# Decay levels of a linear attention: 64 stationary columns, the two halves of the partitions written in turn

## The chip, the cores and the metric

One core of a Trainium2 chip. The metric is the device time of one execution in microseconds (us), taken over several runs of the same program. Engines are named as in the profile: PE is TensorE, PEld its weight load, DVE is VectorE, ACT is ScalarE, POOL is GpSimd, SP is the engine whose queue issues most DMAs.

## What is computed

A decoder trunk of two layers over 256 tokens of width 2048. Layer 0 mixes tokens with a gated linear attention, layer 1 with a forgetting softmax attention; each layer also attends to 256 memory tokens and ends with a gated MLP of width 5632. The change touches the linear attention alone. Cut to that, the reference is:

```python
def step(state, inp):                       # one chunk of 64 tokens, 4 chunks, 4 heads, dk = 256
    qc, kc, vc, gc = inp
    bcum = jnp.cumsum(gc, axis=2)
    o_inter = jnp.einsum('bhtk,bhkv->bhtv', qc * jnp.exp(bcum), state)
    rel = bcum[:, :, :, None, :] - bcum[:, :, None, :, :]
    decay = jnp.exp(jnp.where(tri, rel, -jnp.inf))
    att = jnp.einsum('bhtk,bhsk,bhtsk->bhts', qc, kc, decay)
    o_intra = jnp.einsum('bhts,bhsv->bhtv', att, vc)
```

Each product of a query and a key inside a chunk has a decay of its own for every one of the 256 key channels, so `att` isn't one matrix product.

## The kernel before, in words

All large products are weight projections: weights stream in as units of up to 128 x 1024 floats, ACT rounds each unit to the matmul format (`whi`, line 190), DVE makes the rest (`wlo`, line 199), and PE multiplies both with the activations. Lines 224, 225 and 227 are the products of a projection whose output stands feature by feature (`proj_fm`), lines 261 to 263 those of one whose output stands token by token (`proj_tm`). `split_unit` gives the two casts a high priority; otherwise a scheduler with a cost model of its own lays out one order for each engine, and PE runs its instructions in that order.

The linear attention (`gla`) takes four heads in turn. For each head the projections of q, k and v are followed by `core`, whose work the scheduler spreads between the projections of the next heads. `core` builds the transposed attention matrix `at` (keys on the 128 partitions, queries along the columns) out of these parts, all in plain 32-bit floats:

- line 548: products of the later with the earlier half of the tokens, 128 stationary columns;
- line 552: products of neighbouring chunks inside a half `b` of the tokens, 64 stationary columns, all written to partitions 0 to 63;
- line 557: plain products of each 128-token block with itself, 128 stationary and 128 moving columns, of which line 562 keeps the diagonal by a predicated copy with the identity as mask;
- line 588, for each of three decay levels (`LEVELS`, blocks of 64, 16 and 4 tokens): a block is cut in four, and three versions of the decayed queries (`VERSIONS`, made at lines 572 to 575 as `gdd`) are multiplied with the keys decayed to the end of their quarter (`ks`, lines 581 to 583). The moving side holds the versions of both chunks of a 128-token block, 192 columns (`NVER`), against 128 stationary key columns. Line 595 picks the valid entries with three predicated copies for each level, by a 0/1 mask that `_constants` lays out.

A plain 32-bit matmul is recorded in the profile as two passes, each with a weight load of its own. [...] Lines 602 and 603 multiply `at` with v.

Of the kernel before, what the change touches and what calls it, by code (L numbers as in the profile page):

```python
# [12 lines left out]
F32 = mybir.dt.float32  # L13
F32R = mybir.dt.float32r
I32 = mybir.dt.int32
AF = mybir.ActivationFunctionType
# [3 lines left out]
P = 128  # L20
T = 256
# [9 lines left out]
BIG = 1e30  # L31
PARTS = ((0, 16), (16, 32), (32, 44))

LEVELS = (64, 16, 4)
VERSIONS = ((0, 96), (96, 64), (160, 32))
NVER = 192
NUNIT = 1024
AHEAD = 300

# [97 lines left out]
def _trunk(ctx: ExitStack, tc: tile.TileContext, xt, xtok, memt, wp, wgu, gns, gfin, cnv, par, msk, out):  # L137
    nc = tc.nc
    where, _ = _layout()
    V, S, TE = nc.vector, nc.scalar, nc.tensor  # L140
# [13 lines left out]
    ident = mask[:, M_ID : M_ID + P]  # L154
# [314 lines left out]
    def gla(nx):  # L469
        h, mix = bufB, bufA  # L470
        with tc.tile_pool(name="gla", bufs=1) as gp:
# [53 lines left out]
            def core(hd, q, k, v, bc):  # L525
                at = att[hd % 2]
                e1 = gp.tile([P, 2, T], F32, name="ge1", tag="ed", bufs=2)
                d1 = gp.tile([P, 2, T], F32, name="gd1", tag="ed", bufs=2)
                q1 = gp.tile([P, 2, T], F32, name="gq1", tag="gq1")
                k1 = gp.tile([P, 2, T], F32, name="gk1", tag="gk1")  # L530
                et = sm.tile([P, 2, 2], F32, name="get", tag="get")
                S.activation(et, bc[:, :, 127:192:64], AF.Exp, scale=1.0 / TAU)
                S.activation(e1[:, :, :192], bc[:, :, 64:], AF.Exp, scale=1.0 / TAU)
                V.tensor_tensor(q1[:, :, :192], q[:, :, 64:], e1[:, :, :192], ALU.mult)
                b4 = bc.rearrange("p d (c t) -> p d c t", t=64)
                d4 = d1.rearrange("p d (c t) -> p d c t", t=64)
                V.tensor_tensor(d4[:, :, :3, :], b4[:, :, :3, 63:64].to_broadcast([P, 2, 3, 64]), b4[:, :, :3, :],
                                ALU.subtract)
                S.activation(d1[:, :, :192], d1[:, :, :192], AF.Exp, scale=1.0 / TAU)
                V.tensor_tensor(k1[:, :, 192:], k[:, :, :64], d1[:, :, :64], ALU.mult)  # L540
                V.tensor_tensor(k1[:, :, 64:192], k[:, :, 64:192], d1[:, :, 64:192], ALU.mult)
                for c in range(2):
                    V.tensor_scalar(k1[:, c, :64], k1[:, c, 192:], et[:, c, 0:1], None, ALU.mult)
                    V.tensor_scalar(q1[:, c, 192:], q1[:, c, 128:192], et[:, c, 1:2], None, ALU.mult)
                ps = work("s", 2)
                for c in range(2):
                    mov = q1[:, c, :].rearrange("p (n t) -> p n t", t=64)[:, 1:4:2, :]
                    TE.matmul(ps[:, :P], k1[:, c, :P], mov, start=c == 0, stop=c == 1)
                for b in range(2):
                    for c in range(2):  # L550
                        lhs = k1[:, c, 128:192] if b else k1[:, c, 192:]
                        TE.matmul(ps[:64, P + 64 * b : P + 64 * (b + 1)], lhs, q1[:, c, P * b : P * b + 64],
                                  start=c == 0, stop=c == 1)
                for b in range(2):
                    for c in range(2):
                        bs = slice(b * P, (b + 1) * P)
                        TE.matmul(ps[:, T + b * P : T + (b + 1) * P], k[:, c, bs], q[:, c, bs],  # L557
                                  start=c == 0, stop=c == 1)
                a3 = at.rearrange("p (b t) -> p b t", t=P)[:, 0:3:2, :]
                S.activation(at[:, P : 2 * P], ps[:, :P], AF.Copy)  # L560
                S.activation(a3[:64, :, 64:], ps[:64, P : 2 * P].rearrange("p (b t) -> p b t", t=64), AF.Copy)
                V.copy_predicated(a3, ident.bitcast(I32).unsqueeze(1).to_broadcast([P, 2, P]),
                                  ps[:, T:].rearrange("p (b t) -> p b t", t=P))
                for li, B in enumerate(LEVELS):
                    H = B // 4
                    ps = work("s", 2)
                    dd = gp.tile([P, 4, NVER], F32, name="gdd", tag="gdd")
                    b4, q4 = (t.rearrange("p d (b n t) -> p (d b) n t", b=2, t=B) for t in (bc, q))
                    parts = [(dd[:, :, o : o + w].rearrange("p a (n t) -> p a n t", t=(3 - i) * H), (i + 1) * H)
                             for i, (o, w) in enumerate(VERSIONS)]  # L570
                    for d, t0 in parts:
                        V.tensor_tensor(d, b4[:, :, :, t0:], b4[:, :, :, t0 - 1 : t0].to_broadcast(d.shape), ALU.subtract)
                    S.activation(dd, dd, AF.Exp, scale=1.0 / TAU)
                    for d, t0 in parts:
                        V.tensor_tensor(d, d, q4[:, :, :, t0:], ALU.mult)
                    if H > 1:
                        kt = ks[li % 2]
                        de = gp.tile([P, 2, T], F32, name="gde", tag="ed", bufs=2)
                        b5, k5, e5, kt5 = (t.rearrange("p d (n r t) -> p (d n) r t", r=4, t=H)[:, :, :3, :]
                                           for t in (bc, k, de, kt))  # L580
                        V.tensor_tensor(e5, b5[:, :, :, H - 1 :].to_broadcast(e5.shape), b5, ALU.subtract)
                        S.activation(e5, e5, AF.Exp, scale=1.0 / TAU)
                        V.tensor_tensor(kt5, k5, e5, ALU.mult)
                    else:
                        kt = k
                    for b in range(2):
                        for c in range(2):
                            TE.matmul(ps[:, b * NVER : (b + 1) * NVER], kt[:, c, b * P : (b + 1) * P],  # L588
                                      dd[:, 2 * c + b, :], start=c == 0, stop=c == 1)
                    p3 = ps[:, : 2 * NVER].rearrange("p (b c) -> p b c", b=2)  # L590
                    m3 = mask[:, M_LVL + NVER * li : M_LVL + NVER * (li + 1)].bitcast(I32)
                    for i, (o, w) in enumerate(VERSIONS):
                        o4 = a3.rearrange("p b (n t) -> p b n t", t=B)[:, :, :, (i + 1) * H :]
                        m4 = m3[:, o : o + w].rearrange("p (n t) -> p n t", t=(3 - i) * H).unsqueeze(1)
                        V.copy_predicated(o4, m4.to_broadcast(o4.shape),
                                          p3[:, :, o : o + w].rearrange("p b (n t) -> p b n t", t=(3 - i) * H))
                nrm = Norm(DV, "o")
                os = []
                for j in range(3):
                    po = work("o")  # L600
                    vs = slice(j * P, (j + 1) * P)
                    TE.matmul(po[:, :T], v[:, 0, vs], at[:, :T], start=True, stop=False)  # L602
                    TE.matmul(po[:, P:T], v[:, 1, vs], at[:, T:], start=False, stop=True)
                    o = gp.tile([P, T], F32, name="onorm", tag="onorm", bufs=9)
                    on[3 * hd + j] = o
                    S.activation(o, po[:, :T], AF.Copy)
                    nrm.add(o)
                    os.append(o)
                for j, o in enumerate(os):
                    f = C_GN + 3 * hd + j  # L610
                    V.scalar_tensor_tensor(o, o, part[:, f : f + 1], nrm.row(), ALU.mult, ALU.mult)
# [12 lines left out]
            for hd in range(GLA_H):  # L624
                bc = gates(hd)
                q = gp.tile([P, 2, T], F32, name="gq", tag="gq", bufs=2)
                k = gp.tile([P, 2, T], F32, name="gk", tag="gk", bufs=2)
# [175 lines left out]
    n, then = preparing("ffn0", bufB)  # L803
# [52 lines left out]
def _constants():  # L856
    m = np.zeros((P, M_N), np.float32)
    r = np.arange(P)
    m[:, M_ID : M_ID + P] = np.eye(P)
    m[:, M_ONE : M_ONE + P] = 1.0  # L860
    m[:, M_FOX + P : M_FOX + T] = np.where(r[None, :] > r[:, None], BIG, 0.0)
    m[:, M_SCAN : M_SCAN + T] = np.where(np.arange(T) % 64 == 0, 0.0, 1.0)[None, :]
    for li, B in enumerate(LEVELS):
        for i, (o, w) in enumerate(VERSIONS):
            seg = np.arange(w) // ((3 - i) * B // 4)
            c = M_LVL + NVER * li + o
            m[:, c : c + w] = (r[:, None] // B == seg[None, :]) & (r[:, None] % B // (B // 4) == i)
    return m


# [49 lines left out]
```

## Time and profile before

| | |
|---|---|
| median of 3 runs | 2309.28 us (2309.21 to 2309.69) |
| profiled execution, own time | 2308.97 us |
| its span | 2307.2 us |
| PE busy | 2289.1 us, 12256 passes |
| DVE busy | 1605.6 us |
| ACT busy | 1251.5 us |
| granted PE clock | 0.999 |
| stretch of the linear attention's `core` | about 181 to 400 us |

The page gives busy time by engine, the time in slices, the chain of work that ended last (followed back from the last instruction to what released it) and the costliest groups of instructions. In the group rows, "128\*128 128x192 f32" is a stationary operand of 128 rows and 128 columns, and an output of 128 partitions by 192 columns. In the chain, a row is a start in us, a length in us, engine, tile and line, and the number of passes: the lengths add up without overlap, so the length over the number of passes is the pitch at which passes follow each other, while a pass's own duration in the other views includes the time in the pipe.

### The profile page before, as it was taken

What the parts mean: (1) busy time and instruction counts of PE and PEld (TensorE: products, weight loads), DVE (VectorE), ACT (ScalarE), POOL (GpSimd) and SP (SyncE); (2) the same over time, 40 slices, a digit from 0 to 9 for tenths busy, and PEclk for the clock granted to TensorE, in tenths of its full rate; (3) what the DMA queues carried; (4) which work ended last, traced back from release to release, by engine and by line L of the source; (5) the groups of instructions that cost most, each with busy time, mean ns of one, the idle gap of its engine ahead of it and who ended that gap; (6) DMA issues with size and microseconds to landing.
All of it is one profiled execution on the core that took longest, in us unless ns stands there. A gap on an engine that the chain in (4) does not pass through costs nothing.

```text
span 2307.2 us, 32826 instructions
## 1 busy us (share of the span) xinstructions
PE 2289.1 (99%) x12256; PEld 1986.0 (86%) x12256; DVE 1605.6 (70%) x2595; ACT 1251.5 (54%) x1954; POOL 3.0 (0%) x19
## 2 busy tenths in 40 slices
PE   8999999999999999999999999999999999999998
PEld 7889998888888888888888998888888888888886
DVE  7567877577774777557767557657776577756775
ACT  6555555455553555445565455556554455534554
POOL 0000000000000000000000000000000000000000
PEclk9999999999999999999999999999999999999999
DMA  8655455655555555655555564565556555565554
GB/s 305 204 161 158 147 163 166 192 185 185 190 192 191 192 186 189 192 192 191 187 186 184 172 207 151 163 198 183 191 186 192 194 187 191 186 196 190 186 191 155
DMA packets 124744, 430.27 MB, mean 186 GB/s; under 512 B 14108, under 2 KB 18600, under 8 KB 124456
## 3 DMA queue, kind: packets, MB, share of 16 engines
q1 hardware_dynamic: 124296, 427.65, 57.6%
q8 instruction: 96, 1.57, 0.3%
q10 hardware_dynamic: 288, 0.52, 0.1%
q14 instruction: 64, 0.52, 0.1%
HBM read 426.01 MB, written 2.11 MB: 186 GB/s over the span
## 4 chain that ended last, share of the span: by engine, by line
PE 98%; DMA 0%; ACT 0%; DVE 0%; issue 0%; SPq 0%; DVEq 0%; ACTq 0%
PE acc L224 37%; PE acc L225 20%; PE acc L262 12%; PE acc L263 12%; PE acc L261 12%; PE acc L227 2%; PE ps_s L588 1%; PE ps_s L794 0%; PE ps_t L379 0%; PE ps_s L386 0%; PE ps_o L397 0%; DMA mt<-memt 0%; PE ps_s L708 0%; PE ps_o L602 0%; PE ps_o L724 0%; PE ps_s L557 0%
## 5 line engine op out<-in xcount | busy, mean ns | idle before, releaser
L199 DVE TENSOR_TENSOR wlo<-raw,whi 128x1024 fp32r<-128x1024 f32 (+4 forms) x809 | 972.6, 1203 | 554.1 <-ACT whi L190 541.4
L190 ACT ACTIVATE whi<-raw 128x1024 fp32r<-128x1024 f32 (+4 forms) x809 | 843.2, 1043 | 779.6 <-PE acc L263 366.6
L224 PE MATMUL acc<-B,whi 128*128 128x512 f32 x1980 | 683.4, 395 | 0.0
L224 PE MATMUL acc<-A,whi 128*128 128x512 f32 x1680 | 580.6, 396 | 7.4 <-ACT whi L190 7.4
L225 PE MATMUL acc<-B,wlo 128*128 128x256 f32 x2112 | 551.4, 281 | 0.0
L225 PE MATMUL acc<-A,wlo 128*128 128x256 f32 x1792 | 464.5, 281 | 0.5 <-DVE wlo L199 0.5
L224 PEld LDWEIGHTS acc<-B,whi 128*128 128x128 f32 x1980 | 361.0, 188 | 68.3
L225 PEld LDWEIGHTS acc<-B,wlo 128*128 128x128 f32 x2112 | 397.6, 188 | 20.8
L224 PEld LDWEIGHTS acc<-A,whi 128*128 128x128 f32 x1680 | 305.8, 188 | 64.0 <-ACT whi L190 7.7
L225 PEld LDWEIGHTS acc<-A,wlo 128*128 128x128 f32 x1792 | 338.1, 189 | 21.0 <-DVE wlo L199 1.2
L262 PE MATMUL acc<-wlo,B 128*128 128x512 f32 (+3 forms) x736 | 275.4, 374 | 1.2 <-DVE wlo L199 1.2
L263 PE MATMUL acc<-whi,B 128*128 128x512 f32 (+3 forms) x736 | 273.7, 372 | 0.0
L261 PE MATMUL acc<-whi,B 128*128 128x512 f32 (+3 forms) x736 | 247.8, 372 | 0.0
L262 PE MATMUL acc<-wlo,A 128*128 128x512 f32 x544 | 212.4, 390 | 0.0
L263 PE MATMUL acc<-whi,A 128*128 128x512 f32 x544 | 212.0, 390 | 0.0
L261 PE MATMUL acc<-whi,A 128*128 128x512 f32 x544 | 192.8, 391 | 0.0
L232 ACT ACTIVATE part<-acc 128x256 f32<-128x256 f32 x240 | 90.1, 375 | 165.4 <-PE acc L227 165.4
L262 PEld LDWEIGHTS acc<-wlo,B 128*128 128x128 f32 x736 | 138.2, 188 | 20.6 <-DVE wlo L199 1.5
L263 PEld LDWEIGHTS acc<-whi,B 128*128 128x128 f32 x736 | 138.2, 188 | 18.9
L261 PEld LDWEIGHTS acc<-whi,B 128*128 128x128 f32 x736 | 137.4, 188 | 18.7
L234 DVE TENSOR_TENSOR wholes<-acc,part 128x256 f32<-128x256 f32 x240 | 101.0, 421 | 67.4 <-ACT part L232 67.3
L263 PEld LDWEIGHTS acc<-whi,A 128*128 128x128 f32 x544 | 102.1, 188 | 21.2
(196 smaller groups left out, 1576.1 us busy)
## 6 DMA issues: line engine op xcount, KB each, us to landing
raw<-wp SPq DMA_DIRECT2D x743, 512.0 KB, 3.4
raw<-wp SPq DMA_DIRECT2D x32, 384.0 KB, 3.1
raw<-wp SPq DMA_DIRECT2D x24, 388.0 KB, 3.1
raw<-wp SPq DMA_DIRECT2D x8, 400.0 KB, 3.1
xf<-xt SPq DMA_DIRECT2D x16, 128.0 KB, 4.7
x<-xtok SPq DMA_DIRECT2D x4, 512.0 KB, 7.1
mt<-memt SPq DMA_DIRECT2D x3, 512.0 KB, 7.8
cb<-cdram SPq DMA_DIRECT2D x12, 128.0 KB, 3.4
```

What stands on the lines that cost most here:

```text
L190: casts.append(S.activation(hi[:, s], raw[:, s], AF.Copy))
L199: V.tensor_tensor(lo[:, s], raw[:, s], hi[:, s].bitcast(F32), ALU.subtract)
L224: TE.matmul(a, hi[:, s], both, start=done == 0, stop=False)
L225: TE.matmul(a[:, :T], lo[:, s], both[:, 0, :], start=False, stop=False)
L227: TE.matmul(a, hi[:, s], both, start=False, stop=True)
L232: S.activation(t, a[:, T:], AF.Copy)
L234: V.tensor_tensor(r, a[:, :T], t, ALU.add)
L261: TE.matmul(a, xk[:, 0, xs], hi[:, s], start=u == 0 and j == 0, stop=False)
L262: TE.matmul(a, xk[:, 0, xs], lo[:, s], start=False, stop=False)
L263: TE.matmul(a, xk[:, 1, xs], hi[:, s], start=False, stop=last)
L588: TE.matmul(ps[:, b * NVER : (b + 1) * NVER], kt[:, c, b * P : (b + 1) * P], dd[:, 2 * c + b, :], start=c == 0, stop=c == 1)
```

## The change

Lines 548 and 602 stay. The parts at lines 552, 557 and 588 now use 64 stationary columns throughout, and consecutive matmuls write partitions 0 to 63 and 64 to 127 in turn. A 64-token chunk of keys meets only the decayed queries of its own chunk, so a level's moving side has 96 columns and not 192, and there are eight matmuls where there were four. The diagonal has eight matmuls of 64 moving columns where it had four of 128. The four products of neighbouring chunks keep their size; the second block's go to the upper partitions, and the loops over `b` and `c` are exchanged. Behind them, each predicated copy becomes two of 64 partitions (for a level six in place of three), and the ACT copy of line 561 becomes two. The masks shrink from 192 to 96 columns a level. The decayed queries have the same number of elements, cut as 8 x 96 and not 4 x 192.

```diff
 LEVELS = (64, 16, 4)
-VERSIONS = ((0, 96), (96, 64), (160, 32))
-NVER = 192
+VERSIONS = ((0, 48), (48, 32), (80, 16))
+NVER = 96
...
-                for b in range(2):
-                    for c in range(2):
+                for c in range(2):
+                    for b in range(2):
                         lhs = k1[:, c, 128:192] if b else k1[:, c, 192:]
-                        TE.matmul(ps[:64, P + 64 * b : P + 64 * (b + 1)], lhs, q1[:, c, P * b : P * b + 64],
+                        TE.matmul(ps[64 * b : 64 * (b + 1), P : P + 64], lhs, q1[:, c, P * b : P * b + 64],
                                   start=c == 0, stop=c == 1)
                 for b in range(2):
                     for c in range(2):
-                        bs = slice(b * P, (b + 1) * P)
-                        TE.matmul(ps[:, T + b * P : T + (b + 1) * P], k[:, c, bs], q[:, c, bs],
-                                  start=c == 0, stop=c == 1)
+                        for g in range(2):
+                            gs = slice(b * P + 64 * g, b * P + 64 * (g + 1))
+                            TE.matmul(ps[64 * g : 64 * (g + 1), T + b * 64 : T + (b + 1) * 64], k[:, c, gs], q[:, c, gs],
+                                      start=c == 0, stop=c == 1)
...
-                S.activation(a3[:64, :, 64:], ps[:64, P : 2 * P].rearrange("p (b t) -> p b t", t=64), AF.Copy)
-                V.copy_predicated(a3, ident.bitcast(I32).unsqueeze(1).to_broadcast([P, 2, P]),
-                                  ps[:, T:].rearrange("p (b t) -> p b t", t=P))
+                for b in range(2):
+                    S.activation(a3[:64, b, 64:], ps[64 * b : 64 * (b + 1), P : P + 64], AF.Copy)
+                for g in range(2):
+                    gs = slice(64 * g, 64 * (g + 1))
+                    og = a3[gs, :, gs]
+                    V.copy_predicated(og, ident[gs, gs].bitcast(I32).unsqueeze(1).to_broadcast(og.shape),
+                                      ps[gs, T : T + P].rearrange("p (b t) -> p b t", t=64))
...
-                    dd = gp.tile([P, 4, NVER], F32, name="gdd", tag="gdd")
-                    b4, q4 = (t.rearrange("p d (b n t) -> p (d b) n t", b=2, t=B) for t in (bc, q))
+                    dd = gp.tile([P, 8, NVER], F32, name="gdd", tag="gdd")
+                    b4, q4 = (t.rearrange("p d (g n t) -> p (d g) n t", g=4, t=B) for t in (bc, q))
...
                     for b in range(2):
                         for c in range(2):
-                            TE.matmul(ps[:, b * NVER : (b + 1) * NVER], kt[:, c, b * P : (b + 1) * P],
-                                      dd[:, 2 * c + b, :], start=c == 0, stop=c == 1)
+                            for g in range(2):
+                                TE.matmul(ps[64 * g : 64 * (g + 1), b * NVER : (b + 1) * NVER],
+                                          kt[:, c, b * P + 64 * g : b * P + 64 * (g + 1)],
+                                          dd[:, 4 * c + 2 * b + g, :], start=c == 0, stop=c == 1)
...
                     for i, (o, w) in enumerate(VERSIONS):
                         o4 = a3.rearrange("p b (n t) -> p b n t", t=B)[:, :, :, (i + 1) * H :]
-                        m4 = m3[:, o : o + w].rearrange("p (n t) -> p n t", t=(3 - i) * H).unsqueeze(1)
-                        V.copy_predicated(o4, m4.to_broadcast(o4.shape),
-                                          p3[:, :, o : o + w].rearrange("p b (n t) -> p b n t", t=(3 - i) * H))
+                        for g in range(2):
+                            gs = slice(64 * g, 64 * (g + 1))
+                            n = 64 // B
+                            og = o4[gs, :, g * n : (g + 1) * n, :]
+                            m4 = m3[gs, o : o + w].rearrange("p (n t) -> p n t", t=(3 - i) * H).unsqueeze(1)
+                            V.copy_predicated(og, m4.to_broadcast(og.shape),
+                                              p3[gs, :, o : o + w].rearrange("p b (n t) -> p b n t", t=(3 - i) * H))
```

More of the change, by code (lines that the diff above doesn't have):

```diff
@@ L866, in _constants @@
             c = M_LVL + NVER * li + o
-            m[:, c : c + w] = (r[:, None] // B == seg[None, :]) & (r[:, None] % B // (B // 4) == i)
+            m[:, c : c + w] = (r[:, None] % 64 // B == seg[None, :]) & (r[:, None] % B // (B // 4) == i)
     return m
```

## The prediction

> **What bounds the kernel now.** I read the page first: the busy times, then the chain that ended last.
>
> ```profile
> span 2307.2 us, 32826 instructions
> PE 2289.1 (99%) x12256; PEld 1986.0 (86%) x12256; DVE 1605.6 (70%) x2595; ACT 1251.5 (54%) x1954; POOL 3.0 (0%) x19
> ...
> PE 98%; DMA 0%; ACT 0%; DVE 0%; issue 0%; SPq 0%; DVEq 0%; ACTq 0%
> ```
>
> PE is busy for 99% of the span and is 98% of the chain. Next come PE's waits, over the whole span, and the busy times of the stretch in which the changed code runs.
>
> ```profile
> engine line waited for: us in total, times, longest us
> PE acc L224 <- ACT whi L190: 7.4, 1, 7.4
> PE acc L262 <- DVE wlo L199: 1.2, 1, 1.2
> PE acc L225 <- DVE wlo L199: 0.5, 1, 0.5
> ...
> 181.00:400.00 219.00, 219.00 (x1287) 199.66 (x1286) 174.44 (x386) 121.68 (x206) 0.00 (x0) 1.00 0.50 157
> ```
>
> The columns of the last row are PE, PEld, DVE, ACT and POOL, then the granted clock (1.00). From 181 to 400 us PE has no gap, and none of the three waits is in the changed code. So a nanosecond of PE in `core` is a nanosecond of the end, and the question is what the new matmuls cost PE. The chain, asked for single stretches, prices the old ones (start us, length us, passes):
>
> ```profile
> 181.84 0.45 PE ps_s L548 x4
> 182.29 0.61 PE ps_s L552 x8
> 182.90 1.09 PE ps_s L557 x8
> 183.98 1.30 PE ps_s L588 x8
> 194.00 1.30 PE ps_s L588 x8
> ...
> 225.62 0.49 PE ps_s L552 x6
> 226.12 0.64 PE ps_t L315 x4
> 226.76 0.26 PE ps_s L552 x2
> 227.01 1.09 PE ps_s L557 x8
> ...
> 329.19 0.26 PE ps_s L552 x2
> 329.45 0.38 PE acc L262
> 329.83 0.17 PE acc L263
> ...
> 334.28 0.38 PE ps_s L552 x4
> ...
> 363.36 1.30 PE ps_s L588 x8
> ```
>
> A level (line 588) is 1.30 us for 8 passes of 192 moving columns: 0.1625 a pass. Line 548 gives 0.45 / 4 = 0.112 for 128 stationary and 128 moving columns. Line 552 (64 and 64) gives (0.49 - 0.26) / 4 = 0.0575 from its stretches of 6 and 2 passes. That leaves 0.61 - 8 x 0.0575 = 0.15 and 0.26 - 2 x 0.0575 = 0.145 over: the price of coming into 64 columns. Going out costs too: 1.09 - 8 x 0.112 = 0.19 at line 557, 0.64 - 0.45 = 0.19 at line 315, 0.38 - 0.17 = 0.21 at a projection. A visit to 64 columns thus costs 0.145 + 0.195 = 0.34 us. The passes show half of why:
>
> ```profile
> L552 PE MATMUL ps_s<-gq,gk x32: 222/222/270, 182.2 to 334.4; 128*64 128x64 f32 x32
> L557 PE MATMUL ps_s<-gq,gk x32: 272/275/377, 182.8 to 341.8; 128*128 128x128 f32 x32
> L588 PEld LDWEIGHTS ps_s<-gdd,ks x64: 187/190/192, 183.7 to 354.1; 128*128 128x128 f32 x64
> ```
>
> Durations are minimum, median, maximum in ns. The longest is the first pass behind a switch, which shows its weight load: 270 - 222 = 48 ns for 64 columns, 377 - 275 = 102 for 128. In the rest of the visit, 0.34 - 0.15 = 0.19, no pass starts, half of it on the way in and half on the way out. Inside a level no load shows: loads of 190 ns lie under passes that follow each other every 162.5 ns.
>
> **The change, part by part.**
>
> *Visits.* Before has seven stretches of 64 columns (the chain's rows of line 552, the first at 182.29, the last at 334.28). In the built order of the changed kernel there are 20: three for head 0, four each for heads 1 and 2, nine for head 3, where the scheduler puts projection matmuls between the diagonal and the first level's products. 13 more at 0.34: +4.4 us. This is the surest term, since PE keeps its program order.
>
> *Levels.* A level becomes 16 passes of 96 moving columns. Between 0.0575 at 64 and 0.1625 at 192 the line gives 0.083 at 96. If the halves run one after another, 16 x 0.083 = 1.33 us, +0.03 a level, +0.3 for the 12. If passes of different halves run at the same time, two share a slot of 0.083; the two passes of a matmul go to the same half and queue, so the first of them and the last have no partner: 9 slots, 0.75 us, -0.55 a level, -6.6 in all.
>
> *Diagonal.* 16 passes of 64 and 64 for 8 of 128 and 128: one after another 0.92 against 0.90, +0.1 over four heads; side by side 9 x 0.0575 = 0.52, -0.38 each, -1.5.
>
> *Products of neighbouring chunks.* 8 passes as before; side by side 5 x 0.0575 = 0.29 against 0.46, -0.7 over four heads; else nothing.
>
> No row of before shows two halves at work together, as line 552 writes the lower one alone. So the parts on PE lie between +4.4 + 0.4 = +4.8 us and +4.4 - 6.6 - 1.5 - 0.7 = -4.4 us. With no slot lost at the ends it would be +4.4 - 12 x 0.65 - 4 x 0.45 - 4 x 0.23 = -6.1. With no gain in the two small parts, where load and pass are equally long, +4.4 - 6.6 = -2.2. I take -4.4. [...]
>
> [...]
>
> *DVE and ACT.* 40 predicated copies become 80.
>
> ```profile
> L595 DVE COPY_PREDICATED att<-mask,ps_s 128x192 f32<-128x192 int32 x12 | 4.8, 398 | 4.9 <-PE ps_s L588 4.9
> L595 DVE COPY_PREDICATED att<-mask,ps_s 128x64 f32<-128x64 int32 x12 | 3.6, 298 | 0.1
> L562 DVE COPY_PREDICATED att<-mask,ps_s 128x256 f32<-128x256 int32 x4 | 1.8, 442 | 2.5 <-ACT att L561 2.5
> L561 ACT ACTIVATE att<-ps_s 64x128 f32<-64x128 f32 x4 | 1.0, 258 | 0.0
> 189.13 1.09 DVE L575 TENSOR_TENSOR gdd<-gdd,gq 128x384 f32<-128x384 f32 x3
> ```
>
> 100 ns for 128 more columns: an added copy costs at most its fixed part, 298 - 50 = 0.25 us, so 40 x 0.25 = 10 us is the upper end, added to 174.44 busy in 219. It hides. The queries of head 0's second level are ready at 189.13 + 1.09 = 190.2 and PE reaches them at 194.0: 3.8 us of slack, against 3 x 0.25 = 0.75 more for the copies of the level ahead of them. In the DVE queue the casts (`wlo`) and the next level's subtractions stand behind the copies; PE waits for `wlo` nowhere in this stretch. The four added ACT copies are at most 0.26 us each. If this cover failed, each level could give back up to 0.75 us, 9 us in all; I take nothing. The smaller masks shorten one early load that is none of PE's three waits. Behind `core` the built order is the same.
>
> **The sum.** Against the profiled execution, 2308.97 us: 2308.97 - 4.4 = 2304.6. The median of the runs is 0.31 higher, so 2304.9. That is -0.19%; 0.2%, about what a measurement of this kernel can tell from no change, is 4.6 us.
>
> **The rivals.**
>
> *One after another (slower).* The halves never overlap: a pass of one half starts when the pass of the other has been fed. Then the visits are unpaid: 2309.3 + 4.8 = 2314.1, and up to 2316.5 if PE also waits a little at head 3. It decides from the point where a level, its visit left out, takes more than 1.30 - 4.4 / 12 = 0.93 us: there the levels no longer pay for the visits. For it: no row shows overlap, and one stream of moving columns sets every pitch above. Against it: only the lower half was ever used.
>
> *Loads in turn.* Passes overlap but weight loads of 64 columns go one at a time. If loads run ahead freely, a pass costs 0.0575: 16 x 0.0575 = 0.92 a level, -4.6, with +0.1 for the diagonal and +4.4 for visits: -0.1, 2309.2. If a load starts only when the pass before it starts, pitches alternate between 0.083 and 0.0575, 1.12 a level: -2.2 + 0.1 + 4.4 = +2.3, 2311.6.
>
> *Every change of half shows (slower).* About 35 changes of half a head (3 in the products, 8 in the diagonal, 8 in each level), 140 in all. If each shows a weight load of 48 ns, +6.7 on +4.8: 2320.8. If each also empties the array, 0.145 as on the way in: +20.3 on +4.8, 2334.4. Against it: the load of the next pass hides within one half, and the price above belongs to a change of size.
>
> [...]
>
> *DVE becomes the bound (slower).* The 0.75 us a level appear as PE waits: up to +9 on top of -4.4, 2313.9. Against it: the slack of 3.8 us.
>
> That the change doesn't do what it says is ruled out: the built program alternates the halves.
>
> **How the numbers follow.** Side by side 0.44, with its own range 2303.2 to 2307.1 (the ends -6.1 and -2.2); as its centre lies 0.2 us from the bound, I split it, 0.22 faster and 0.22 within. Loads in turn 0.10, within. One after another 0.27, of which 0.07 within, as +4.8 is close to the bound too, and 0.20 slower. Every change shows 0.14, slower. DVE 0.05, slower. Faster 0.22, same 0.39, slower 0.39. The range runs from the best case, with 0.7 us below it for the noise of the prices, 2302.5, to the upper end of one after another, 2316.5; beyond it lie the 0.14 and nothing else of weight.
>
> **What would show it.** In the profile after, the chain should give a level as about 0.75 us plus up to 0.34, and passes of 64 stationary columns should start in pairs, the lower half's and the upper half's closer together than 0.083. A level of 1.33 plus 0.34 shows one after another, 0.92 the loads, over 1.7 a price at each change of half. Visits should be 20 at 0.34. A PE wait in 181 to 400 us would show that DVE was not covered. The forecast is wrong if the chain's length for lines 588 and 557 together doesn't fall by about 8 us before visits are counted.

## The result, and the profile after

The changed kernel takes 2304.34 us (median of 13 runs, 2303.8 to 2305.75) against 2309.23 for the kernel before: a ratio of 0.9979 with a 95% interval of 0.9972 to 0.9986, that is 4.9 us faster (3.2 to 6.5). The forecast was 2304.9. Line numbers of the changed kernel are one higher than before's up to the changed code and twelve higher behind the levels; in the experiments they shift again, and the tile names tell what a row is.

The page after, its first lines and the chain by engine:

```profile
span 2302.3 us, 33124 instructions
PE 2284.6 (99%) x12384; PEld 1976.7 (86%) x12384; DVE 1614.8 (70%) x2635; ACT 1253.2 (54%) x1958; POOL 3.0 (0%) x19
PE 99%; DMA 0%; ACT 0%; DVE 0%; issue 0%; SPq 0%; DVEq 0%; ACTq 0%
```

PE still is the chain; its 128 more passes are the 64 more matmuls. Its waits, and the busy times of the changed stretch (the second row ends 5 us earlier, as the work does):

```profile
PE acc L225 <- ACT whi L191: 7.2, 2, 5.8
PE acc L263 <- DVE wlo L200: 1.3, 1, 1.3
PE acc L226 <- DVE wlo L200: 0.5, 1, 0.5
...
181.00:400.00 219.00, 219.00 (x1436) 194.15 (x1435) 186.89 (x433) 125.91 (x214) 0.20 (x4) 1.00 0.51 160
181.00:395.00 214.00, 214.00 (x1414) 190.01 (x1413) 183.04 (x427) 123.22 (x211) 0.00 (x0) 1.00 0.51 161
```

The same three kinds of wait, and again no gap of PE in the stretch. DVE has 183.04 where it had 174.44. The chain through the changed code (start us, length us, passes; 549 is the old line 548, 553 the products, 559 the diagonal, 595 a level):

```profile
181.81 0.44 PE ps_s L549 x4
182.26 0.38 PE ps_s L553 x8
182.64 0.47 PE ps_s L559 x16
183.10 0.66 PE ps_s L595 x16
183.77 0.31 PE acc L226
...
184.79 0.12 PE acc L226
...
192.86 0.81 PE ps_s L595 x16
201.40 0.81 PE ps_s L595 x16
...
322.40 0.26 PE ps_s L559 x2
325.39 0.27 PE ps_s L559 x4
```

Head 0's first visit holds products, diagonal and first level. The diagonal's 16 passes take 0.47 us where one after another would be 0.92, the level's 16 take 0.66 where it would be 1.33: two passes to a slot (the pitch of single passes: 0.0575 in the kernel before, and 0.083, estimated so far, as the lower-then-upper run below has it). A level in a visit of its own is 0.81, the 0.66 and 0.15 for coming in; going out is 0.31 - 0.12 = 0.19 at line 226. So a visit still costs 0.34. The two last rows show the pairs from the other side: in head 3 a visit with one matmul (2 passes, one half) takes 0.26, a visit with two matmuls (both halves) 0.27. The second matmul costs 0.01.

The pairs can also be seen one by one. The timeline of PE in the level at 192.79, up to 192.798, 192.803, 192.93 and 192.94 us (start us, length us, and how many passes have begun by then):

```profile
192.79 0.30 PE L595 MATMUL ps_s<-gdd,ks 128*64 128x96 f32 x1
192.79 0.30 PE L595 MATMUL ps_s<-gdd,ks 128*64 128x96 f32 x2
192.79 0.38 PE L595 MATMUL ps_s<-gdd,ks 128*64 128x96 f32 x3
192.79 0.39 PE L595 MATMUL ps_s<-gdd,ks 128*64 128x96 f32 x4
```

The second pass has begun within 9 ns of the first. By the starts in the trace it is 6 ns, and 7 ns from the third to the fourth.

The ledger, from these rows and those of before: levels 12 x (1.30 - 0.66) = -7.7 us; diagonal 4 x (0.90 - 0.47) = -1.7; products 4 x (0.46 - 0.23) = -0.9; 13 more visits at 0.345 = +4.5; and 8 of the 20 visits hold an odd number of matmuls, whose last has no partner, 0.05 to 0.08 each, +0.45. The sum is -5.4; the span fell by 4.9. The remaining 0.5 us is on no row of its own, and less than the interval of the ratio.

### The profile page after: what moved, and what is told of

Same layout as the page of the kernel before. It is cut to its first block, busy times and chain, and to the rows that moved or that the text cites. A ratio compares the mean times of both kernels' runs of the same rounds, so it can differ in the third digit from the quotient of the medians.

```text
span 2302.3 us, 33124 instructions
## 1 busy us (share of the span) xinstructions
PE 2284.6 (99%) x12384; PEld 1976.7 (86%) x12384; DVE 1614.8 (70%) x2635; ACT 1253.2 (54%) x1958; POOL 3.0 (0%) x19
## 4 chain that ended last, share of the span: by engine, by line
PE 99%; DMA 0%; ACT 0%; DVE 0%; issue 0%; SPq 0%; DVEq 0%; ACTq 0%
PE acc L225 37%; PE acc L226 20%; PE acc L263 12%; PE acc L264 12%; PE acc L262 12%; PE acc L228 2%; PE ps_s L806 0%; PE ps_s L595 0%; PE ps_t L380 0%; PE ps_s L387 0%; PE ps_o L398 0%; DMA mt<-memt 0%; PE ps_s L720 0%; PE ps_o L614 0%; PE ps_o L736 0%; PE ps_s L514 0%
```

## The experiments

Theory: passes of 64 stationary columns that write different halves of the partitions run at the same time, as 0.66 us for 16 of them in the changed kernel suggests, and the price is the visits. Against it stand that the order of the halves has nothing to do with it, that only large passes gain, and that DVE's doubled copies matter.

**Lower half first, then upper.** In all three groups the loop over the halves goes outermost; for the levels:

```diff
-                    for b in range(2):
-                        for c in range(2):
-                            for g in range(2):
+                    for g in range(2):
+                        for b in range(2):
+                            for c in range(2):
                                 TE.matmul(ps[64 * g : 64 * (g + 1), b * NVER : (b + 1) * NVER],
```

> The changed kernel with the loops over the halves put outermost: in each group (products, diagonal, each level) all matmuls of the lower half come first, then all of the upper. The same 144 matmuls with 64 stationary columns, 19 visits. Theory (halves overlap only where passes of different halves stand next to each other in the order): one after another again, a level 16 x 0.083 = 1.33 us in the chain beside its visit, the diagonal 0.92; 2309.2 + 12 more visits than before x 0.345 + 0.4 = 2313.8 us, slower than before by 0.2%. Rival 1 (the array takes the next pass of a free half from anywhere in its queue): a level stays at 0.66, the time at that of the changed kernel, 2304.3. Rival 2 (64 stationary columns are cheaper by themselves, the halves have nothing to do with it): also 2304.3, but single passes of 96 columns then follow each other at 0.041 and no two start within 0.01 us.

Measured: 2308.18 us, 0.9998 of before (0.9989 to 1.0007). Neither theory's number. A level in the chain, the timeline of PE up to 193.517 and up to 193.524 us, and the durations of such passes (minimum, median, maximum):

```profile
193.20 1.19 PE ps_s L595 x16
...
193.13 0.63 PE L595 MATMUL ps_s<-gdd,ks 128*64 128x96 f32 x5
193.13 0.69 PE L595 MATMUL ps_s<-gdd,ks 128*64 128x96 f32 x6
...
L595 PE MATMUL ps_s<-gdd,ks x128: 246/246/298, 182.9 to 353.3; 128*64 128x96 f32 x128
```

1.19 - 0.15 = 1.04 us: neither 1.33 nor 0.66. Five passes have begun by 193.517 us, six by 193.524. The five begin 0.083 apart, (0.63 - 0.246 - 0.05) / 4, with 0.05 more behind the first. The sixth ends at 193.13 + 0.69 = 193.82 and so lasts about 0.30 us, as the longest passes do, 298 ns for 246. The trace doesn't name the half of a pass. Line 552 of before writes one half, and of its visit at 182.29 one pass is longer than the rest, the first, 270 ns for 222. In the changed kernel, which writes both, the first two are: 297 ns each in the level at 192.79, and the other 14 take 246. So I read a longer pass as the first of its half, and the sixth here as the first upper one, ninth in the order, ahead of the lower passes six to eight. Four lower slots alone, then eight with the upper half: 12 x 0.083 + 0.05 = 1.05. So in this run passes of different halves overlapped that weren't next to each other in the order: the free half took its pass from four places further on, and not from five or more, as the first four lower passes ran alone. That the halves have nothing to do with it falls: the same matmuls in another order cost 4.4 us more by the ratios, and the levels alone are 12 x 0.38 = 4.6 longer.

**Two lower, two upper.** The new theory was put to a test in which the half changes after every four passes.

```diff
                     for b in range(2):
-                        for c in range(2):
-                            for g in range(2):
+                        for g in range(2):
+                            for c in range(2):
```

> The changed kernel, with the half of a level's matmuls changing after every second matmul (four passes) and not after every one. Theory from the lower-then-upper run (a half that is free takes its next pass from at most four passes further on in the order: there the first upper pass started with the fifth of eight lower ones): the first upper pass, fifth in the order, starts with the first lower one, and a level stays at 0.66 us plus its visit, 0.81 in the chain. Rival (a pass starts only behind all that stand before it in the order): the four lower passes are half through before the upper ones start, 12 slots of 0.083 or more, 1.0 to 1.1 in the chain.

```profile
193.34 0.86 PE ps_s L595 x16
...
193.28 0.30 PE L595 MATMUL ps_s<-gdd,ks 128*64 128x96 f32 x1
193.28 0.31 PE L595 MATMUL ps_s<-gdd,ks 128*64 128x96 f32 x2
```

The second row goes up to 193.28 us, the third up to 193.29: two passes have begun within 0.01 us, where two of one half were 0.083 apart, so the fifth in the order, the first upper one, begins with the first. A level is 0.86 for 0.81, not 1.0 to 1.1; the 0.05 more is about half a slot, and no row here places it. The one run took 2304.65 us. The strict order falls; a reach of four passes fits.

**The small parts alone.** The kernel before with the new products and diagonal, and the old levels.

> The kernel before with the products of neighbouring chunks and the diagonal alone in alternating halves of 64 columns; the three levels stay at 128 stationary and 192 moving columns. 10 visits where before has 7. Theory: the two small parts are worth as much as the levels, pass for pass: diagonal 4 x (0.90 - 8 x 0.058 = 0.43) = 1.7, products 4 x 0.23 = 0.9, visits +3 x 0.345 = 1.0: -1.6, 2307.6 us. Rival (where a load takes as long as its pass the loads go one at a time, and these parts gain nothing): +1.0 + 0.1, 2310.3.

Measured: 2307.07, 0.9994 (0.9985 to 1.0003), -1.4 us, for -1.6 forecast. The interval nearly reaches the rival's 1.0005, so the chain decides:

```profile
181.41 0.38 PE ps_s L552 x8
181.79 0.47 PE ps_s L558 x16
182.26 1.50 PE ps_s L593 x8
```

The diagonal is 0.47 in this kernel too, for 16 passes with a load each: 0.029 a load, where line 552 before had 0.0575. In the changed kernel's trace the loads of the diagonal also begin in pairs, 6 to 7 ns apart, each recorded as 132 to 138 ns. The old level behind it is 1.50, its 1.30 and the way out.

**The copies alone.** The kernel before with 80 predicated copies in place of 40, nothing else; at the levels:

```diff
-                        V.copy_predicated(o4, m4.to_broadcast(o4.shape),
-                                          p3[:, :, o : o + w].rearrange("p b (n t) -> p b n t", t=(3 - i) * H))
+                        pv = p3[:, :, o : o + w].rearrange("p b (n t) -> p b n t", t=(3 - i) * H)
+                        mv4 = m3[:, o : o + w].rearrange("p (n t) -> p n t", t=(3 - i) * H)
+                        for g in range(2):
+                            gs = slice(64 * g, 64 * (g + 1))
+                            n = slice(g * (64 // B), (g + 1) * (64 // B))
+                            og = o4[gs, :, n, :]
+                            V.copy_predicated(og, mv4[gs, n, :].unsqueeze(1).to_broadcast(og.shape), pv[gs, :, n, :])
```

> The kernel before, with each predicated copy cut in two copies of 64 partitions and the ACT copy in two, as in the changed kernel; all matmuls, masks and visits as before. Theory (the 40 added copies hide behind PE): 2309.2, within 0.05% of before, no PE wait in 181 to 400 us, DVE busy there up by 5 to 10 us. Rival (DVE's added work delays a later PE input): up to +9 us, 2318, with PE waits in that stretch.

Measured: 2308.84, 1.0001 (0.9992 to 1.001). The stretch:

```profile
181.00:400.00 219.00, 219.00 (x1286) 199.57 (x1285) 183.34 (x426) 122.07 (x210) 0.00 (x0) 1.00 0.47 157
```

DVE 183.34 for 174.44, 8.9 us more or 0.22 a copy, and PE without a gap: the cover holds at this size.

**Quarters.** The two fine levels take 32 stationary columns, and the copies there double again. In the cut, `G` is the number of parts, `C` their stationary and `W` their moving columns.

```diff
+PARTN = (2, 4, 4)
...
-                            for g in range(2):
-                                TE.matmul(ps[64 * g : 64 * (g + 1), b * NVER : (b + 1) * NVER],
+                            for g in range(G):
+                                TE.matmul(ps[C * g : C * (g + 1), b * W : (b + 1) * W],
```

> The changed kernel with the levels of blocks of 16 and 4 tokens in quarters: 32 stationary columns, 48 moving columns, 16 matmuls a level that write partitions 0, 32, 64 and 96 onwards in turn, and twice the predicated copies there; 20 visits as in the changed kernel. Theory (parts of the array's columns work side by side, four as well as two): 32 passes in 8 slots of 48 x 0.00082 + 0.004 = 0.043: 0.34 a level for 0.66, -0.32 x 8 = -2.6: 2301.8 us. Rival 1 (there is room for two passes at a time, not for four): 16 slots of 0.043 = 0.69, 2304.5. Rival 2 (passes can't be issued faster than the 7 ns at which pairs start now, or the loads of 32 columns show): 32 x 0.025 = 0.8 a level, +1.1, 2305.4.

Measured: 2303.66, 0.9979 (0.9971 to 0.9988): by its time, no gain on the changed kernel. The trace says otherwise of PE. A level in the chain, the timeline of PE up to 192.953 us, PE's waits in the stretch and its busy times:

```profile
193.00 0.48 PE ps_s L598 x32
...
192.93 0.25 PE L598 MATMUL ps_s<-gdd,ks 128*32 128x48 f32 x4
...
PE ps_t L349 <- DVE dg L347: 1.5, 1, 1.5
PE ps_o L617 <- DVE att L610: 0.2, 1, 0.2
...
181.00:400.00 219.00, 217.14 (x1566) 191.41 (x1565) 193.46 (x481) 125.68 (x214) 0.20 (x4) 1.00 0.48 161
```

0.48 - 0.15 = 0.33 for 32 passes: four to a slot, eight slots of 0.041 us, where 0.043 was estimated for 48 moving columns. PE has the forecast gain in its passes, and of these 2.6 us DVE takes back 1.9: it is busy for 193.46 us, and PE idle for 219 - 217.14. The other 0.7 is on no row, and less than the interval.

The timeline also bounds the reach. Each quarter has two passes in a row, and four passes have begun within 0.02 us, half a slot. If no quarter gave two of them, the fourth is the seventh in the order and begins with the first. That is six places on, not four. What the three runs have in common is the number of passes ahead that had not begun: the sixth to eighth in the lower-then-upper order, the second to fourth in two and two, the second, fourth and sixth here, three each time. Whether passes are counted or matmuls of two passes, no run here parts.

**Quarters with fewer copies.** The copies of the upper two quarters are left out, 12 a head, and with them half of the fine levels' entries: a kernel that only serves to find the cause.

> The quarters kernel without the predicated copies of the upper two quarters of its two fine levels: 192 fewer elements' worth of copies a head are left out, so half of these levels' entries never reach the attention matrix. DVE then has as many copies as in the changed kernel (80), and shorter ones. The built order has 23 visits for 20. Theory (the quarters' gain was given back to PE waits behind DVE's added copies): no PE wait in 181 to 400 us, and 2.6 - 3 x 0.35 = 1.5 us under the changed kernel, 0.9972 of before. Rival (the gain of the quarters goes elsewhere): the same as the quarters, 0.9979, with its waits.

Measured: 2301.84, 0.9972 (0.9961 to 0.9983), as the theory had it.

```profile
181.00:400.00 219.00, 219.00 (x1570) 193.41 (x1569) 184.46 (x433) 126.99 (x214) 0.20 (x4) 1.00 0.49 162
```

PE is without a gap again. The difference to the quarters before is within the intervals of both; the two rows of PE's busy time speak for the cause. They don't leave it alone: the built order changed too (23 visits for 20), and this run doesn't part the two.

**Ten visits.** The matmuls of a head are gathered in two visits: with the first level the diagonal and the products, then the other two levels together. `tc.issue_after` keeps the others behind the first matmul of the level that is ready last.

```diff
+                with tc.high_priority(offset=AHEAD):
...
+                    with tc.issue_after(level(ps[:, 320:], kt, dd).ins):
...
+                two = [prepare(1), prepare(2)]
+                pl = work("s", 2)
+                with tc.high_priority(offset=AHEAD):
+                    with tc.issue_after(level(pl[:, 192:384], *two[1]).ins):
+                        level(pl[:, :192], *two[0])
```

> The changed kernel with the matmuls gathered: the first level, the diagonal and the products in one visit of a head, the second and third levels in another; 10 visits in the built order for 20. For that the decayed queries have two buffers, the small tiles of the attention four for five and one gate weight buffer for two. Same matmuls, same copies. Theory (a visit costs 0.345 us, and the seven stretches with an odd number of matmuls some 0.05 more each): -10 x 0.345 - 0.4 = -3.9 on the changed kernel, 0.9962 of before, about 2300.4 us. Rival (the inputs of two levels at once, and fewer buffers, let PE wait for DVE, which is 85% busy in that stretch): PE waits of 2 to 5 us, 2302 to 2305.

The changed kernel was run beside it.

> The changed kernel as it is, on the chip of the runs beside it: 0.9979 of the kernel before, 20 visits of 0.345 us.

Measured: ten visits 2300.12, 0.9962 (0.9949 to 0.9975); the changed kernel 2303.7, 0.9977 (0.9967 to 0.9986). Ten visits fewer are worth 3.6 us, 0.36 each; in this are also four visits with an odd number of matmuls where there were eight, and a PE wait of 0.4 us on ACT in the stretch. The chain shows a first visit and a second one with two levels:

```profile
186.28 0.81 PE ps_s L574 x16
187.09 0.46 PE ps_s L606 x16
187.56 0.23 PE ps_s L611 x8
194.24 1.47 PE ps_s L574 x32
```

1.47 for two levels, where they were 0.81 each, and their second way out is gone too. It beats both kernels, and is the fastest here that leaves nothing out.

**Ten visits with quarters, and with fewer copies.**

> The same with the second and third levels in quarters of 32 stationary columns. Theory: PE's passes -2.6 on the ten visits, but 96 more predicated copies of 0.2 us on DVE less the shorter ones; where the quarters on the changed kernel gave nothing because PE waited for DVE, the same holds here: between -2.6 and +1 on the ten visits, 2298 to 2301.5, with a PE wait behind DVE at the first head. Rival (with fewer visits DVE's work is no longer in the way): the full -2.6, 2297.8, and no PE wait in 181 to 400 us.

> The ten-visit kernel with quarters, with the same copies of the upper two quarters left out; 10 visits as in the ten-visit kernel. Theory (DVE's copies made PE wait where quarters and ten visits were together): the waits for wlo and att in 181 to 400 us shrink to under 1 us, and the time falls 2.6 us under the ten-visit kernel, 0.9951 of before, about 2297.5. Rival (quarters in one visit of two levels delay the casts by themselves): the waits stay, 2304 to 2307.

Measured: 2307.36, 0.9993 (0.9984 to 1.0001) with all copies, worse than both theories and 7 us over the ten visits; 2298.07, 0.9956 (0.9943 to 0.9968) with the copies left out. PE's waits, first with all copies, then with fewer:

```profile
PE acc L264 <- DVE wlo L201: 7.2, 6, 2.1
PE ps_o L642 <- DVE att L599: 1.7, 2, 1.2
```

```profile
PE acc L264 <- DVE wlo L201: 1.4, 2, 1.1
```

The casts `wlo` stand in DVE's queue behind its other work, the copies among it. With all copies, PE waits for casts six times and for the last copies twice. One of the six waits, and 1.1 of the 1.4 us left with fewer copies, is the wait near 1315 us that all kernels have; the others, 5.1 us with all copies and 0.3 with fewer, lie in the stretch. So the copies make them: both kernels have ten visits, cut nearly alike. The quarters add 48 copies (2683 DVE instructions for 2635), not the 96 that were expected. I had bounded this loss by the one PE wait of the quarters alone, but DVE had little room left. From 200 to 300 us, first the ten visits with halves, then with quarters and all copies:

```profile
200.00:300.00 100.00, 99.50 (x678) 90.68 (x677) 96.25 (x245) 60.96 (x110) 0.00 (x0) 1.00 0.49 162
200.00:300.00 100.00, 94.47 (x708) 84.09 (x707) 95.67 (x254) 57.88 (x103) 0.00 (x0) 1.00 0.45 148
```

DVE is 96% busy in both; the first still keeps PE at work, and with more copies PE stands still for 5.5 us.

## Why the prediction was right, step by step

*PE is the end.* Right, and shown from both sides: what the passes saved arrived in the time where PE had no gap (219.00 us busy of 219, the span 4.9 us shorter), and in part did not arrive where PE waited for DVE (quarters: 217.14 of 219, 2303.66 us).

*Side by side.* Right: pairs 6 to 7 ns apart, 16 passes in eight slots. The choice was the author's estimate, at 0.44, and one after another at 0.27: no row of before had decided it. What the runs show is passes for different halves 6 to 7 ns apart, and passes for one half 0.083 us apart (lower-then-upper). The lower-then-upper run shows that the gain hangs on the order of the matmuls, 1.04 us a level for 0.66, and the change has this order right. The sign that was named, lines 588 and 557 shorter by about 8 us, came as 7.7 + 1.7 = 9.4.

*The size of a level.* The step that missed: "the first of them and the last have no partner: 9 slots". It assumed that a pass waits for all before it in the order. In the changed kernel passes of the free half came forward, so the pairs began at once: 8 slots, 0.66 for 0.75 a level, and likewise 0.47 for 0.52 and 0.23 for 0.29. These terms together were -8.8 and measured -10.3. The prediction had this case as its other end, -6.1, and didn't take it. Its end of -2.2 took load and pass of the small parts as equally long, which no run shows: in the trace a load is 138 ns and a pass 222, and the small parts gained 1.7 + 0.9.

*Visits.* The price, 0.34, and the count, 20, were right. PE kept the built order of the visits, 20 in the chain as in the program; within a level it did not keep that of the passes: in the lower-then-upper run six had begun by 193.524 us, the sixth read as the ninth in the order. Missing was that a visit with an odd number of matmuls leaves one alone, +0.45. This and the 0.5 us that no row holds cancel most of the gain above, so -4.4 met -4.9 closer than its terms did. That part is luck.

*DVE hidden.* Right: 8.9 us of copies cost nothing. The rival with DVE as the bound did not hold here, but what it describes appeared when the copies of two levels doubled again: PE was idle for 219 - 217.14 = 1.9 us. The upper end of the range, 2316.5, rested on PE waiting a little at head 3, for which no row gave a size; PE had no gap there.

*Every change of half shows.* Wrong by the pairs. 16 passes whose half changes after every second one took 0.66 us, eight slots. Of a level in a visit of its own only the first pass of each half was longer, 297 ns for 246, and the diagonal's 16 loads went into 0.47 us. The 0.145 of the way in did not come back at a change of half.

## What to carry to other kernels

Where, as in the levels here, half of what a matmul computes is thrown away, try to cut its stationary side and alternate the halves: in plain 32-bit floats two passes of 64 columns took the slot of one (16 in 0.66 us), and so did four of 32 (32 in 0.33 us). Count the visits before the passes: each stretch of 64 columns cost 0.34 us, and the 13 added ones 4.5 of the 10.3 us gained here, so gather such matmuls. Then look at who reads the results: copies cut by partitions cost no time while DVE had room (183.34 us busy of 219), and where it was already 96% busy, the next ones brought PE waits of 6.8 us.

## What was not expected of the hardware

A free half took a pass from further on in the order: in the lower-then-upper run the ninth pass is read as the one that began within 0.01 us of the fifth, and with quarters the seventh as the one that began within 0.02 us of the first. Read so, it overtook three passes that had not begun, and not more, in these runs. A visit with one matmul took 0.26 us, and a visit with a second one in the other half 0.27.
